# A decoder block in fp32: the convolution's shifted copies through DRAM, second operands and layer-norm factors in PSUM banks, no layer-norm end on GpSimd

## The chip, the cores and the metric

The kernel runs on one core of a Trainium2 chip. The metric is the device time of one execution in microseconds (us); the lower, the better.

## The reference, cut to what matters

One decoder layer over 256 tokens of 2048 channels, in fp32. The part that the change touches is the mixing sub-layer, where one input projection feeds two groups.

```python
z = rms_norm(x) @ w_in                       # 2048 -> 3360 + 2 * 1024 columns
# RWKV group: every column is shifted, z + (prev - z) * mu, then r, k, v of 8 pairs of heads
kk = kk / max(sqrt(sum(kk * kk)), 1e-12)     # norm of the keys, per head
y = wkv7_scan(...)                           # the recurrence; then group norm, gain, bias, bonus, gate
# convolution group
u = u_lin * sigmoid(u_gate)                  # 1024 channels
c = depthwise_conv(u, width 31) + dw_b
c = (c - mean(c)) * rsqrt(var(c) + 1e-5) * ln_gain + ln_bias     # over the channels
y_conv = c * sigmoid(c)
mixed = concat(y, y_conv) @ w_out            # then a residual, an MLP of 8192, an embedding gate
```

## The kernel before, in words

All activations lie transposed, channels on the partitions and the 256 tokens along the free axis. A matrix product of a weight tile (128 output channels, 16 blocks of 128 input channels) is made of three fp32r products: weight and activation are each split into a high and a low part. SP's queue loads 1 MB of weights into one of two buffers `W`; in four quarters ScalarE casts the high part `wh` (L285), and mostly GpSimd subtracts it to get the low part `wl` (L248); TensorE runs the tile (L434 to L442) into one of two PSUM banks `acc`. A tile of w_in is 48 matmuls.

The work is written as generators that ask for buffers (`Take`) and issue operations; a planner (`Plan.run`) with a cost for each operation decides the order on every engine while the program is built, and engine queues keep this order. An operation releases its buffers when it is through. Operations may name two engines, of which the planner takes the one that is done first (`PD` and `DP` are GpSimd or VectorE). Tiles of w_in have a low priority and fill TensorE between the pieces of the eight pairs of heads. `ORDER` places the tiles of the pairs and of eight convolution blocks (128 channels each; one tile `lin`, one `gate`). After the last convolution block comes the layer norm over all 1024 channels, while the tiles of the last pairs still run; then w_out's convolution half, while the last recurrences run; then w_out's other half. At about 510 us the mixing is over, and the MLP follows.

What the change and the prediction speak of, with the lines before:

- `scaled` and `zshift` (L614 to L632): a tile leaves its bank `acc` by a multiplication with the row norm on VectorE into `zp`, which frees the bank; ScalarE writes `(1 - mu) * z` into `zt` in SBUF, and VectorE joins both, with two SBUF operands.
- `keys` (L691 to L722): norms of the keys in `n4`, and their copy `rn` (L714), SBUF to SBUF.
- `inverse`: the small sums `ud` (L838) of each pair, in SBUF.
- `recur` and `group_norm` (L972 to L1002): the recurrence's output is copied by ScalarE from its bank `psy` into `ysb`, and normed from there.
- `ev_gate` (L1021): the gate times `u`, two SBUF operands, on GpSimd or VectorE.
- `taps` (L1034): the block's `u` (128 channels, 3 zeros and 256 tokens) is brought into four groups of 32 channels, each in four shifts on four groups of partitions, by 16 matmuls with columns of the identity (L1044) into two banks `wk`, which ScalarE copies into the one buffer `cv` (L285). 32 matmuls then make the convolution (L1056).
- `layer_norm` (L1065): mean (L1070), squares, variance (L1082), then `1 / sqrt` into `csq` (L1084), and for each block the multiplication by `csq`, gain and bias, a sigmoid on ScalarE and the last product, on GpSimd or VectorE and from SBUF alone.

Of the kernel before, what the change touches and what calls it, by code (L numbers as in the profile page):

```python
# [16 lines left out]
P = 128  # L17
# [37 lines left out]
TAP, LNP, AFP = 4.0, 1.0, 3.5  # L55
# [42 lines left out]
class Plan:  # L98
# [100 lines left out]
    def issue(self, task, best):  # L199
# [123 lines left out]
def decoder_block(ctx: ExitStack, tc: tile.TileContext, x, p, w_in, w_gd, w_out, w_up, w_down,  # L323
# [225 lines left out]
    pl.static("cv", cvst)  # L549
    def v4(t):  # L550
# [63 lines left out]
    def scaled(acc, o, W, cols=P):  # L614
        yield Wait(lambda: "rstd" in S)
        r = S["rstd"]
        yield pl.tt(["DVE"], o, acc.t[:cols, :T], r.t[:cols], ALU.mult, T, [acc, r], [W], [acc])

    def zshift(acc, o, W, mu, j=0, cols=P):
        zp = yield Take("zp", 1)  # L620
        yield pl.memset(zp.t[:, 0:1], 0.0, [(zp, 0)], 1)
        yield from scaled(acc, zp.t[:cols, 1:], zp, cols)
# [69 lines left out]
    def keys(j):  # L692
# [12 lines left out]
        n4 = yield Take("n4")  # L705
        yield pl.ts(["DVE"], n4.t, psn.t[:, 0:4], 1e-24, None, ALU.max, None, 4, [psn], [n4], [psn])
# [88 lines left out]
    def bonus(j):  # L795
# [4 lines left out]
        yield pl.stt(rk.t, zr.t, vec("r_k", j), kp.t, ALU.mult, ALU.mult, T, [zr, kp], [rk], [zr, kp])  # L800
# [713 lines left out]
```

## Time and profile before

| what | us |
|---|---|
| median of 3 runs | 1400.93 (1400.87 to 1402.88) |
| the profiled execution | 1402.03 |
| its span, first to last instruction | 1400.2 |
| TensorE busy | 1351.5 (97%) |
| GpSimd busy | 1174.2 (84%) |
| ScalarE busy | 799.4 (57%) |
| VectorE busy | 736.4 (53%) |

The profiled execution took 1.8 us more than its span and lies 1.1 us above the median. A busy share is over the whole span; what binds a stage is read from the stage's windows, the waits and the chain. TensorE's clock has two levels here, 1.2 and 2.4 GHz; the profile gives the mean as a share of the upper one.

### The profile page before, as it was taken

The numbers are of one execution on the slowest core, as the hardware profiler recorded it, in microseconds if no ns is written. First come the engines' busy times: TensorE is split into PE (matmuls) and PEld (weight loads), VectorE is DVE, ScalarE is ACT, GpSimd is POOL, SyncE is SP. The second block draws the span as 40 slices with busy tenths as digits, with TensorE's granted clock in tenths as the row PEclk, the third lists the DMA queues.
The fourth block names the chain that finished last, engine by engine and source line by source line (L and its number), as shares of the span: only waits on it lengthen the run. The fifth ranks groups of instructions, "written<-read, shape, count | busy, mean of one in ns | idle before, by whom it ended". The sixth has DMA issues, their size and how long they took to land.

```text
span 1400.2 us, 27458 instructions
## 1 busy us (share of the span) xinstructions
PE 1351.5 (97%) x10476; PEld 1182.8 (84%) x10476; DVE 736.4 (53%) x1305; ACT 799.4 (57%) x1667; POOL 1174.2 (84%) x1002
## 2 busy tenths in 40 slices
PE   8999999999789999999999999999999999999898
PEld 7868878788778998788888888888888888889688
DVE  7256837235886545687003663236632266433694
ACT  6835665556657656855445554455554455555853
POOL 7765756576777769789999999999999999999787
PEclk9999999999899999999999999999999999999999
DMA  7442333433222465345555554555554555555353
GB/s 243 159 140 95 115 130 113 137 110 137 91 99 95 153 248 182 128 160 194 211 182 191 194 185 181 183 189 194 187 181 182 187 194 189 181 181 190 124 198 120
DMA packets 40354, 229.40 MB, mean 164 GB/s; under 512 B 6304, under 2 KB 9632, under 8 KB 14624
## 3 DMA queue, kind: packets, MB, share of 16 engines
q1 hardware_dynamic: 40224, 227.66, 46.0%
q8 instruction: 82, 1.34, 0.4%
q14 instruction: 48, 0.39, 0.1%
HBM read 225.55 MB, written 2.10 MB: 163 GB/s over the span
## 4 chain that ended last, share of the span: by engine, by line
PE 86%; DVE 8%; ACT 2%; issue 1%; DMA 1%; POOL 1%; SPq 0%; DVEq 0%; ACTq 0%; POOLq 0%
PE acc L441 34%; PE acc L442 17%; PE acc L434 8%; PE acc L435 7%; PE acc L436 7%; PE acc L440 3%; PE inv L1056 2%; PE acc L439 1%; PE wk L1044 1%; DVE hl L252 1%; DVE acc L246 1%; DVE acc L252 1%; PE psy L930 1%; PE seq L938 1%; PE wk L749 1%
## 5 line engine op out<-in xcount | busy, mean ns | idle before, releaser
L248 POOL TENSOR_TENSOR wl<-W,wh 128x512 fp32r<-128x512 f32 x548 | 734.4, 1353 | 119.2 <-ACT wh L285 99.3
L285 ACT CAST wh<-W 128x512 fp32r<-128x512 f32 x568 | 346.3, 618 | 220.3 <-PE acc L440 69.0
L441 PE MATMUL acc<-hl,wh 128*128 128x512 f32 x1016 | 369.8, 403 | 11.3 <-DVE hl L252 5.7
L441 PE MATMUL acc<-fhl,wh 128*128 128x512 f32 x806 | 288.2, 395 | 0.0
L442 PE MATMUL acc<-hl,wl 128*128 128x256 f32 x1016 | 286.5, 282 | 0.0
L434 PE MATMUL acc<-hl,wh 128*128 128x256 f32 (+1 forms) x928 | 282.1, 304 | 1.0 <-DVE zp L246 0.9
L436 PE MATMUL acc<-hl,wl 128*128 128x256 f32 (+1 forms) x928 | 265.2, 286 | 6.3 <-POOL wl L248 6.0
L435 PE MATMUL acc<-hl,wh 128*128 128x256 f32 (+1 forms) x928 | 265.7, 286 | 3.2 <-DVE hl L252 2.0
L248 POOL TENSOR_TENSOR wl<-Wb,wh 128x512 fp32r<-128x512 f32 x173 | 237.0, 1380 | 18.4 <-ACT wh L285 11.2
L441 PEld LDWEIGHTS acc<-hl,wh 128*128 128x128 f32 x1016 | 192.1, 189 | 60.2 <-DVE hl L252 8.4
L442 PE MATMUL acc<-fhl,wl 128*128 128x256 f32 x806 | 227.2, 282 | 0.0
L442 PEld LDWEIGHTS acc<-hl,wl 128*128 128x128 f32 x1016 | 193.2, 190 | 3.7
L434 PEld LDWEIGHTS acc<-hl,wh 128*128 128x128 f32 (+1 forms) x928 | 179.2, 193 | 15.6 <-issue 10.1
L246 DVE TENSOR_TENSOR gt<-acc,tb 128x256 f32<-128x256 f32 x124 | 52.4, 423 | 263.7 <-ACT tb L276 263.1
L436 PEld LDWEIGHTS acc<-hl,wl 128*128 128x128 f32 (+1 forms) x928 | 179.1, 193 | 7.3 <-POOL wl L248 6.6
L435 PEld LDWEIGHTS acc<-hl,wh 128*128 128x128 f32 (+1 forms) x928 | 179.5, 193 | 5.4 <-DVE hl L252 3.7
L441 PEld LDWEIGHTS acc<-fhl,wh 128*128 128x128 f32 x806 | 151.5, 188 | 33.4
L285 ACT CAST wh<-Wb 128x512 fp32r<-128x512 f32 x174 | 107.6, 621 | 89.4 <-PE acc L440 35.5
L442 PEld LDWEIGHTS acc<-fhl,wl 128*128 128x128 f32 x806 | 151.3, 188 | 2.7
L246 DVE TENSOR_TENSOR f<-f 128x256 f32<-128x256 f32 x63 | 85.9, 1366 | 1.9
L246 DVE TENSOR_TENSOR fhl<-f,fhl 128x256 fp32r<-128x256 f32 x62 | 58.5, 946 | 26.0 <-ACT fhl L276 26.0
L248 POOL TENSOR_TENSOR wlb<-W,whb 128x512 fp32r<-128x512 f32 x50 | 69.2, 1384 | 1.9 <-ACT whb L285 1.6
(319 smaller groups left out, 2004.2 us busy)
## 6 DMA issues: line engine op xcount, KB each, us to landing
W<-in_w_up_dram SPq DMA_DIRECT2D x43, 1024.0 KB, 4.8
W<-in_w_down_dram SPq DMA_DIRECT2D x42, 1024.0 KB, 4.8
W<-in_w_in_dram SPq DMA_DIRECT2D x38, 1024.0 KB, 4.9
Wb<-in_w_down_dram SPq DMA_DIRECT2D x22, 1024.0 KB, 4.8
Wb<-in_w_up_dram SPq DMA_DIRECT2D x21, 1024.0 KB, 4.8
W<-in_w_out_dram SPq DMA_DIRECT2D x14, 1024.0 KB, 4.8
W<-in_w_gate_dram SPq DMA_DIRECT2D x11, 1024.0 KB, 5.0
Wb<-in_w_gate_dram SPq DMA_DIRECT2D x5, 1024.0 KB, 4.8
```

What stands on the lines that cost most here:

```text
L246: alts.append((e, dve, lambda: nc.vector.tensor_tensor(out=out, in0=a, in1=b, op=op), None, pen))
L248: alts.append((e, 220 + 2.27 * n, lambda: nc.gpsimd.tensor_tensor(out=out, in0=a, in1=b, op=op), None, pen))
L252: return Op([("DVE", 210 + 1.042 * n + (0 if self.from_psum(R) or n < 128 else PORT), lambda: self.nc.vector.scalar_tensor_tensor(out=out, ...
L285: alts.append((e, 150 + 0.835 * n, lambda: self.nc.scalar.copy(out, a), None, 0))
L434: return [nc.tensor.matmul(o, h, xk[:, 0, :], start=(i == 0), stop=False), nc.tensor.matmul(o, h, xk[:, 1, :], start=False, stop=False), n ...
L435: nc.tensor.matmul(o, h, xk[:, 1, :], start=False, stop=False),
L436: nc.tensor.matmul(o, l, xk[:, 0, :], start=False, stop=(i == n - 1))]
L439: return [nc.tensor.matmul(a[:cols, T:], l, xk[:, 0, :], start=False, stop=False), nc.tensor.matmul(a[:cols, :], h, both, start=False, sto ...
L440: nc.tensor.matmul(a[:cols, :], h, both, start=False, stop=True)]
L441: return [nc.tensor.matmul(a[:cols, :], h, both, start=(i == 0), stop=False), nc.tensor.matmul(a[:cols, T:], l, xk[:, 0, :], start=False, ...
L442: nc.tensor.matmul(a[:cols, T:], l, xk[:, 0, :], start=False, stop=False)]
L1056: nc.tensor.matmul(ps.t[32 * g:32 * g + 32, :T], cw.t[:, g, m, :], cv.t[:, g, 4 * m:4 * m + T], start=(m == 0), stop=(m == 7)) for g in ra ...
```

## The change

Three things, all between about 60 and 510 us. **The copies:** `taps` no longer uses TensorE and ScalarE to spread `u`; one DMA writes `u` into a buffer in DRAM, and four DMAs read it back, shifted, into `cv`, 40 DMAs in all on SP's queue. The planner charges SP 600 ns for each and 4 us and more until it lands, instead of 60 ns and 330 ns for loads (330 ns now). **Second operands in PSUM:** of two operands on VectorE one now mostly lies in a bank: the shift's second half in the upper half of the tile's own `acc`, the sigmoid of the gate likewise, `psy` directly instead of `ysb`, the bonus joined in a bank, `n4` and `ud` in banks. So banks are held longer: `acc` until the shift is done, `wk` of the norms until `rn` is written, `inv` from the sums on, `wk` instead of `psy` in the group norm. **The end of the layer norm:** the reciprocal goes into the bank `pv`; eight multiplications by it on VectorE; then sigmoid (into a bank `wk`) and gain and bias (in place) both on ScalarE, and the last product on VectorE with the sigmoid in the bank. GpSimd has no part in it. Instructions in all: TensorE 9115 to 8987 (the 128 of L1044), ScalarE 1635 to 1615, GpSimd 1002 to 994, VectorE 1305 to 1309, SP's DMAs 266 to 306.

```diff
@@ Plan.issue
         if eng == "DMA":
-            self.clock["SP"] = st + 60
-            self.dma = max(self.dma, st + 700) + c
-            en = self.dma + 1900
+            self.clock["SP"] = st + (func or 330)
+            if func:
+                en = max(self.dma, st + 700) + c + 3300
+            else:
+                self.dma = max(self.dma, st + 700) + c
+                en = self.dma + 1900
@@ scaled, zshift
-        yield pl.tt(["DVE"], o, acc.t[:cols, :T], r.t[:cols], ALU.mult, T, [acc, r], [W], [acc])
+        yield pl.tt(["DVE"], o, acc.t[:cols, :T], r.t[:cols], ALU.mult, T, [acc, r], [W], [] if keep else [acc])
-        d = yield Take("zt", 1)
-        yield pl.act(d.t[:cols], zp.t[:cols, 1:], AF.Identity, T, [zp, "omu"], [d], scale=om)
-        a, b = zp.t[:cols, 0:T], d.t[:cols]
+        d = acc.t[:cols, T:]
+        yield pl.act(d, zp.t[:cols, 1:], AF.Identity, T, [zp, "omu"], [(acc, "d")], scale=om)
+        a, b = zp.t[:cols, 0:T], d
...
-        yield pl.stt(o, a, mu, b, ALU.mult, ALU.add, T, [d, zp, (zp, 0), "vt"], [W], [d, zp])
+        yield pl.stt(o, a, mu, b, ALU.mult, ALU.add, T, [(acc, "d"), zp, (zp, 0), "vt"], [W], [acc, zp])
@@ keys
-        n4 = yield Take("n4")
-        yield pl.ts(["DVE"], n4.t, psn.t[:, 0:4], 1e-24, None, ALU.max, None, 4, [psn], [n4], [psn])
+        n4, kn = psn.t[:, 4:8], (psn, "n")
+        yield pl.ts(["DVE"], n4, psn.t[:, 0:4], 1e-24, None, ALU.max, None, 4, [psn], [kn])
...
-        yield pl.vec(202, lambda: nc.vector.tensor_copy(rn.t, n4.t[:, :, None].to_broadcast([P, 4, C])),
-                     [n4], [rn], [n4])
+        yield pl.vec(202, lambda: nc.vector.tensor_copy(rn.t, n4[:, :, None].to_broadcast([P, 4, C])),
+                     [kn], [rn], [psn])
@@ inverse
-        ud = yield Take("ud")
+        pe = yield Take("inv")
+        ud, kd = pe.t[:, T:T + 32].rearrange("p (c j) -> p c j", c=NC), (pe, "t")
...
@@ recur, group_norm
-        yield pl.copy(["ACT"], ysb.t.rearrange("p a t -> p (a t)"), psy.t[:, :T], T, [(psy, False), (psy, True)], [ysb], [psy])
-        pl.spawn(group_norm(j, ysb), 1.1)
+        pl.spawn(group_norm(j, psy), 1.1)
...
-        yield pl.tt(["DVE"], cen.t, ysb.t, s4.t[:, :, None].to_broadcast([P, 4, C]), ALU.subtract, T,
-                    [ysb, s4], [cen], [s4])
+        yield pl.tt(["DVE"], cen.t, yv, s4.t[:, :, None].to_broadcast([P, 4, C]), ALU.subtract, T,
+                    ky + [s4], [cen], [s4, psy])
...
-        pgn = yield Take("psy")
+        pgn = yield Take("wk", 2)
...
-        yield pl.stt(y.t[:, j, :], bv.t, vec("gn_bias", j), gs.t, ALU.add, ALU.mult, T, [bv, gs], [(y, j)], [bv, gs])
+        yield pl.stt(y.t[:, j, :], pgn.t[:, T:], vec("gn_bias", j), gs.t, ALU.add, ALU.mult, T, [(pgn, 1), gs], [(y, j)], [pgn, gs])
@@ ev_gate
-            yield pl.act(gt.t, gt.t, AF.Sigmoid, T, [gt], [gt])
+            yield pl.act(acc.t[:, T:], gt.t, AF.Sigmoid, T, [gt], [(acc, "d")], [gt])
...
-            yield pl.tt(PD, lin, lin, gt.t, ALU.mult, T, [gt, u], [u], [gt])
+            yield pl.tt(["DVE"], lin, lin, acc.t[:, T:], ALU.mult, T, [(acc, "d"), u], [u], [acc])
@@ taps
-        for b in range(2):
-            pr = yield Take("wk")
-            for g in (2 * b, 2 * b + 1):
-                o = (g % 2) * T
-                yield pl.pe(600, lambda: [
-                    nc.tensor.matmul(pr.t[32 * i:32 * i + 32, o:o + T], ident[:, 32 * g:32 * g + 32],
-                                     u.t[:, i:i + T], start=True, stop=True) for i in range(4)],
-                            [u, (u, 0), "fc"], [pr], [u] if g == 3 else [])
-            yield pl.copy(["ACT"], cv.t[:, 2 * b:2 * b + 2, 28:], pr.t.rearrange("p (g t) -> p g t", g=2), 2 * T,
-                          [pr], [(cv, b)], [pr])
+        ur = yield Take("ur")
+        yield pl.dma_move(ur.t, u.t, P * (3 + T) * 4, [u, (u, 0)], [ur], [u])
+        for i in range(4):
+            yield pl.dma_move(cv.t[32 * i:32 * i + 32, :, 28:], ur.t[:, i:i + T].rearrange("(g c) t -> c g t", g=4),
+                              P * T * 4, [ur], [(cv, i)] + [cv] * (i == 0), [ur] if i == 3 else [])
@@ layer_norm
-        yield pl.act(csum, pv.t[:, :T], AF.Sqrt, T, [pv], ["csum"], [pv], bias=bias_cache[LN_EPS])
-        yield pl.vec(1669, lambda: nc.vector.reciprocal(csq, csum), ["csum"], ["crs"])
+        yield pl.act(csum, pv.t[:, :T], AF.Sqrt, T, [pv], ["csum"], bias=bias_cache[LN_EPS])
+        rp, kr = pv.t[:, T:], (pv, "r")
+        yield pl.vec(1669, lambda: nc.vector.reciprocal(rp, csum), ["csum"], [kr])
...
-                yield pl.tt(DP, a, a, csq, ALU.mult, T, ["crs", (y, NP + j, "m")], [k])
-                yield pl.ts(DP, a, a, vec("ln_g", j), vec("ln_b", j), ALU.mult, ALU.add, T, [k], [k])
-                g = yield Take("sqt")
-                yield pl.act(g.t, a, AF.Sigmoid, T, [k], [g])
-                yield pl.tt(PD, a, a, g.t, ALU.mult, T, [k, g], [(y, NP + j)], [g])
...
+            lg = yield Take("wk")
+            yield pl.act(lg.t[:, :T], a, AF.Sigmoid, T, [k], [lg], scale=vec("ln_g", j), bias=vec("ln_b", j))
+            yield pl.act(a, a, AF.Identity, T, [k], [(y, NP + j, "l")], scale=vec("ln_g", j), bias=vec("ln_b", j))
+            yield pl.tt(["DVE"], a, a, lg.t[:, :T], ALU.mult, T, [(y, NP + j, "l"), lg], [(y, NP + j)], [lg])
...
+            yield pl.tt(["DVE"], a, a, rp, ALU.mult, T, [kr, (y, NP + j, "m")], [(y, NP + j, "n")], [pv])
```

The planner writes another order with it. Three places matter below. The first is SP's queue at the first convolution block (`cw` are the block's taps, `gup` weights of a pair, `ur` the buffer in DRAM, `cvst` is `cv`), before and then with the change:

```order
L231 DMA cw<-in_w_cv_dram 128x1024
L231 DMA W<-in_w_in_dram 128x2048 x2
L231 DMA gup<-in_w_gup_dram 128x256
L231 DMA W<-in_w_in_dram 128x2048
```

```order
L234 DMA cw<-in_w_cv_dram 128x1024
L234 DMA W<-in_w_in_dram 128x2048
L234 DMA gup<-in_w_gup_dram 128x256
L237 DMA ur<-u 128x259
L234 DMA W<-in_w_in_dram 128x2048
L237 DMA cvst_111<-ur 32x4x256 x4
L234 DMA W<-in_w_in_dram 128x2048
```

The write to DRAM waits in the queue for `u`, and the four reads wait for the write to land; one weight load stands between them, and the next one behind them.

The second is TensorE at the third convolution block, with the change. `acc_2160` is the bank of its gate tile, `acc_2320` and `acc_2499` those of the next two tiles; the rows on `seq` are a recurrence, those on `X` and `U` a pair's inverse:

```order
L441 MATMUL acc_2160<-hl_121,wh_2182 128x256
L442 MATMUL acc_2160<-hl_121,wl_2183 128x256
L440 MATMUL acc_2320<-hl_121,wh_2216 128x256
...
L886 MATMUL inv_2444<-X_2434,U_2139 32x32 x16
L946 MATMUL seq_2457<-SV_1775,arK_1598 128x128
...
L442 MATMUL acc_2499<-hl_121,wl_2450 128x256
L1059 MATMUL inv_2637<-cvst0_111,cw_2294 32x256 x4
L952 MATMUL seq_2703<-rh_2705,xbst0_110 128x64
L1059 MATMUL inv_2637<-cvst0_111,cw_2294 32x256 x8
```

Between the end of the gate tile and the first convolution matmul (L1059) stand 81 matmuls of tiles and pieces of the pairs; at the other seven blocks it is more. The copying matmuls are gone.

The third is GpSimd at the end of the layer norm, before and then with the change (`wl` are weight splits), and VectorE there with the change:

```order
L248 TENSOR_TENSOR wl<-W,wh 128x512
L248 TENSOR_TENSOR y<-y,csq 128x256
L265 TENSOR_SCALAR y<-y,vt 128x256
L248 TENSOR_TENSOR y<-y,csq 128x256 x3
L248 TENSOR_TENSOR y<-y,sqt 128x256
L265 TENSOR_SCALAR y<-y,vt 128x256
L248 TENSOR_TENSOR y<-y,sqt 128x256 x3
L291 MEMSET zp 128x1
L248 TENSOR_TENSOR arK<-zr,Ep 64x4x64
L248 TENSOR_TENSOR BK<-kp,Em 64x4x64
L248 TENSOR_TENSOR wl<-W,wh 128x512 x2
```

```order
L254 TENSOR_TENSOR wl<-W,wh 128x512
L254 TENSOR_TENSOR cen<-cen,s_5047 128x256
L254 TENSOR_TENSOR wl<-W,wh 128x512 x3
L297 MEMSET zp 128x1
L254 TENSOR_TENSOR wl<-W,wh 128x512 x3
L297 MEMSET Ep 128x4
```

```order
L1088 RECIPROCAL wk<-csum 128x256
L258 SCALAR_TENSOR_TENSOR wk<-wk,vt,bv 128x256
L252 TENSOR_TENSOR y<-y,wk 128x256 x8
L258 SCALAR_TENSOR_TENSOR y<-wk,vt,gs 128x256
L252 TENSOR_TENSOR zp<-acc,rstd 128x256
```

The ten pieces of the layer norm that stood between the weight splits are gone from GpSimd's queue; on VectorE the eight multiplications stand in one block ahead of the next tile's `zp`.

## Rows read from the trace of the kernel before

**Rows 1.** Page, part 1 (busy us, share of the span, instructions of two engines) and part 2 (one character for each of 40 slices of 35 us; PEclk in tenths of full speed).

```profile
PE 1351.5 (97%) x10476; PEld 1182.8 (84%) x10476; DVE 736.4 (53%) x1305; ACT 799.4 (57%) x1667; POOL 1174.2 (84%) x1002
...
PEclk9999999999899999999999999999999999999999
```

**Rows 2.** Busy time of each engine in three windows of 35 us, from the end of the convolution's tiles to the start of w_out's (us from the span's start, length, then each engine's busy us with its instructions, the granted clock, the DMA engines' busy share, GB/s).

```profile
350.00:385.00 35.00, 26.25 (x210) 24.69 (x209) 31.41 (x54) 21.57 (x47) 26.28 (x33) 0.87 0.26 91
385.00:420.00 35.00, 30.21 (x356) 27.29 (x356) 30.66 (x71) 19.90 (x46) 27.54 (x31) 0.98 0.28 99
420.00:455.00 35.00, 32.18 (x422) 29.81 (x420) 21.29 (x61) 26.21 (x67) 27.07 (x32) 0.90 0.27 95
```

**Rows 3.** Page, part 4: the chain that ended last, shares of the span by engine.

```profile
PE 86%; DVE 8%; ACT 2%; issue 1%; DMA 1%; POOL 1%; SPq 0%; DVEq 0%; ACTq 0%; POOLq 0%
```

**Rows 4.** Groups of TensorE instructions over the whole span (line, operation, out<-in, shape, count | busy us, mean ns of one | idle just before, releaser). A matrix product in fp32 is two records.

```profile
L1044 PE MATMUL wk<-u,fc 128*32 128x256 f32 x256 | 19.1, 395 | 1.9 <-DVE bv L246 1.9
L1056 PE MATMUL inv<-cvst,cw 128*32 128x256 f32 x512 | 31.8, 383 | 0.0
L878 PE MATMUL inv<-X,U 32*32 32x32 f32 x512 | 7.3, 194 | 0.2 <-ACT cvst L285 0.2
```

**Rows 5.** TensorE in order of time around the first convolution's copies (start us, us, instruction, in brackets the idle time before it and who ended it). Between the first two rows shown lie 36 more matmuls of tiles.

```profile
62.05 0.28 PE L434 MATMUL acc<-hl,wh 128*128 128x256 f32 x1
...
66.48 0.28 PE L435 MATMUL acc<-hl,wh 128*128 128x256 f32 x1
...
73.83 0.64 PE L1044 MATMUL wk<-u,fc 128*32 128x256 f32 x8
...
75.03 0.64 PE L1044 MATMUL wk<-u,fc 128*32 128x256 f32 x8
...
78.80 1.52 PE L1044 MATMUL wk<-u,fc 128*32 128x256 f32 x16 [1.87 <-DVE bv L246]
```

**Rows 6.** Busy time in windows of 5 us, the same columns as in group 2: two at the first convolution's copies, four at the end of the layer norm.

```profile
75.00:80.00 5.00, 3.13 (x34) 1.75 (x33) 3.70 (x4) 1.10 (x2) 4.27 (x4) 0.93 0.14 49
80.00:85.00 5.00, 5.00 (x57) 3.89 (x57) 1.50 (x4) 2.44 (x5) 3.53 (x4) 0.73 0.14 21
370.00:375.00 5.00, 3.46 (x39) 3.06 (x37) 3.56 (x10) 2.47 (x7) 5.00 (x7) 1.00 0.01 2
375.00:380.00 5.00, 1.86 (x7) 1.57 (x7) 5.00 (x6) 1.01 (x3) 4.73 (x6) 0.62 0.09 16
380.00:385.00 5.00, 3.69 (x18) 3.70 (x19) 4.68 (x9) 4.92 (x9) 2.30 (x5) 0.50 0.54 193
385.00:390.00 5.00, 4.42 (x34) 3.97 (x34) 2.19 (x5) 4.08 (x10) 0.57 (x1) 0.85 0.01 2
```

**Rows 7.** TensorE at the end of the layer norm, in order of time.

```profile
377.52 0.58 PE L436 MATMUL acc<-hl,wl 128*128 128x256 f32 x1 [4.06 <-POOL wl L248]
```

**Rows 8.** GpSimd at the end of the layer norm, in order of time.

```profile
364.57 1.29 POOL L248 TENSOR_TENSOR wl<-W,wh 128x512 fp32r<-128x512 f32 x1
365.81 0.92 POOL L248 TENSOR_TENSOR y<-y,csq 128x256 f32<-128x256 f32 x1
...
372.62 2.13 POOL L248 TENSOR_TENSOR y<-y,sqt 128x256 f32<-128x256 f32 x3
...
376.21 2.67 POOL L248 TENSOR_TENSOR wl<-W,wh 128x512 fp32r<-128x512 f32 x2
```

**Rows 9.** Groups of VectorE instructions between 0 and 510 us, columns as in group 4. The first four read two operands in SBUF, the last two one in SBUF and one in a PSUM bank.

```profile
L252 DVE SCALAR_TENSOR_TENSOR zk<-zp,vt,zt 128x256 f32<-128x256 f32 x8 | 6.1, 758 | 6.2 <-ACT zt L277 5.5 <-POOL csq L248 0.7
L252 DVE SCALAR_TENSOR_TENSOR zr<-zp,vt,zt 128x256 f32<-128x256 f32 x8 | 5.9, 734 | 1.7 <-ACT zt L277 1.7
L252 DVE SCALAR_TENSOR_TENSOR vd<-zp,vt,zt 128x256 f32<-128x256 f32 x8 | 7.1, 886 | 0.8 <-ACT zt L277 0.7
L252 DVE SCALAR_TENSOR_TENSOR y<-bv,vt,gs 128x256 f32<-128x256 f32 x8 | 7.2, 901 | 0.2
L252 DVE SCALAR_TENSOR_TENSOR bv<-psy,vt,bv 128x256 f32<-128x256 f32 x8 | 3.9, 482 | 5.2 <-PE psy L994 5.1
L246 DVE TENSOR_TENSOR y<-y,wk 128x256 f32<-128x256 f32 x8 | 3.3, 411 | 0.4 <-PE wk L1070 0.4
```

**Rows 10.** The copy of the key norms from SBUF to SBUF, among the instructions on tile rn (count, ns shortest/median/longest, first and last start).

```profile
L714 DVE COPY rn<-n x8: 293/468/1394, 69.9 to 418.3; 128x256 f32<-128x256 f32 x8
```

**Rows 11.** VectorE in order of time: the two steps of one token shift.

```profile
367.80 0.40 DVE L246 TENSOR_TENSOR zp<-acc,rstd 128x256 f32<-128x256 f32 x1
...
379.91 0.47 DVE L252 SCALAR_TENSOR_TENSOR vd<-zp,vt,zt 128x256 f32<-128x256 f32 x1
```

**Rows 12.** DMA issues on SP's queue (count, KB each, median us from issue to landing).

```profile
out_dram<-os SPq DMA_DIRECT2D x16, 128.0 KB, 1.8
gup<-in_w_gup_dram SPq DMA_DIRECT2D x8, 128.0 KB, 5.1
pt<-in_p_dram SPq DMA_DIRECT2D x1, 256.0 KB, 9.8
```

**Rows 13.** The first convolution's gate tile: VectorE's first step on it and GpSimd's last, in order of time.

```profile
69.52 0.42 DVE L246 TENSOR_TENSOR gt<-acc,rstd 128x256 f32<-128x256 f32 x1 [0.99 <-PE acc L436]
...
71.06 0.69 POOL L248 TENSOR_TENSOR u<-u,gt 128x256 f32<-128x256 f32 x1
```

More of the change, by code (lines that the diff above doesn't have):

```diff
@@ L549, in decoder_block @@
     pl.static("cv", cvst)
+    dr = pa.enter_context(tc.tile_pool(name="dr", bufs=2, space=bass.MemoryType.DRAM))
+    reg(dr, "ur", 2, [P, 3 + T])
     def v4(t):
@@ L612, in x_norm, with scaled @@
         yield pl.act(warm, bias_cache[1e-6], AF.Sigmoid, 1, (), ["warm"])
-    def scaled(acc, o, W, cols=P):
+    def scaled(acc, o, W, cols=P, keep=False):
         yield Wait(lambda: "rstd" in S)
         r = S["rstd"]
-        yield pl.tt(["DVE"], o, acc.t[:cols, :T], r.t[:cols], ALU.mult, T, [acc, r], [W], [acc])
+        yield pl.tt(["DVE"], o, acc.t[:cols, :T], r.t[:cols], ALU.mult, T, [acc, r], [W], [] if keep else [acc])
     def zshift(acc, o, W, mu, j=0, cols=P):
@@ L621, in zshift @@
         yield pl.memset(zp.t[:, 0:1], 0.0, [(zp, 0)], 1)
[L622 removed]
+        yield from scaled(acc, zp.t[:cols, 1:], zp, cols, True)
         mu, om = vec(mu, j, rows=cols), omu[:cols, VOFF[mu] + j if VOFF[mu] < 24 else 24 + VOFF[mu] - VOFF["mu_wa"] + j:][:, 0:1]
[L624 to L626 removed]
+        d = acc.t[:cols, T:]
+        yield pl.act(d, zp.t[:cols, 1:], AF.Identity, T, [zp, "omu"], [(acc, "d")], scale=om)
+        a, b = zp.t[:cols, 0:T], d
         if len(o.shape) == 3:
             a, b = ck(a), ck(b)
[L629 removed]
+        yield pl.stt(o, a, mu, b, ALU.mult, ALU.add, T, [(acc, "d"), zp, (zp, 0), "vt"], [W], [acc, zp])
     def ev_wa(acc):
@@ L836, in inverse @@
                     m8[:, None, :, None].to_broadcast(sh), ALU.mult, T, Uk + ["fc"], [um])
-        ud = yield Take("ud")
-        yield pl.vec(335, lambda: nc.vector.tensor_reduce(out=ud.t, in_=um.t.rearrange("p c q j -> p c j q"),
-                                                          axis=mybir.AxisListType.X, op=ALU.add), [um], [ud], [um])
+        pe = yield Take("inv")
+        ud, kd = pe.t[:, T:T + 32].rearrange("p (c j) -> p c j", c=NC), (pe, "t")
+        yield pl.vec(555, lambda: nc.vector.tensor_reduce(out=ud, in_=um.t.rearrange("p c q j -> p c j q"),
+                                                          axis=mybir.AxisListType.X, op=ALU.add), [um], [kd], [um])
         udh = yield Take("udh")
         udl = yield Take("udl")
-        yield pl.copy(["DVE"], udh.t, ud.t, 32, [ud], [udh])
-        yield pl.tt(["DVE"], udl.t, ud.t, udh.t.bitcast(F32), ALU.subtract, 32, [ud, udh], [udl], [ud])
+        yield pl.copy(["DVE"], udh.t, ud, 32, [kd], [udh])
+        yield pl.tt(["DVE"], udl.t, ud, udh.t.bitcast(F32), ALU.subtract, 32, [kd, udh], [udl])
         es = []
@@ L1023, in f @@
             gt = yield Take("gt")
-            yield from scaled(acc, gt.t, gt)
-            yield pl.act(gt.t, gt.t, AF.Sigmoid, T, [gt], [gt])
+            yield from scaled(acc, gt.t, gt, keep=True)
+            yield pl.act(acc.t[:, T:], gt.t, AF.Sigmoid, T, [gt], [(acc, "d")], [gt])
             yield Wait(lambda: "u" in cvs[j])
@@ L1057, in taps @@
                                  start=(m == 0), stop=(m == 7)) for g in range(4)],
-                        [cw, (cv, 0), (cv, 1)], [ps], [cw, cv] if m == 7 else [])
+                        [cw] + [(cv, i) for i in range(4)], [ps], [cw, cv] if m == 7 else [])
         yield pl.act(a, ps.t[:, :T], AF.Identity, T, [ps], [ka], [ps], bias=vec("dw_b", j))
```

40 lines of the change are left out of this document (21 added, 19 removed).

## The prediction

> **What bounds the kernel now.** I read the page's shares and slices first, then the chain, then windows of the stages that the diff touches, and last the waits in them.
>
> TensorE is busy 97% of the span [rows 1], and it makes up 86% of the chain that ended last, VectorE 8% and GpSimd 1% [rows 3]. So a matmul that goes away is worth its time wherever TensorE runs without a gap, and another engine's work is worth something only where TensorE waits for it. It waits in few places. The worst stretch is 350 to 455 us [rows 2]: TensorE is busy 26.25, 30.21 and 32.18 of 35 us, so 16.4 us are lost to gaps, while VectorE is at 31.4 and 30.7 of 35 in the first two windows. There the layer norm ends beside the last tiles of w_in.
>
> The heart of it is 370 to 390 us [rows 6]. Idle are 1.54, 3.14, 1.31 and 0.58 us, together 6.6. After the gap the granted clock is 0.62, 0.50 and 0.85 of full speed (0.50 is the lower level, 1.2 GHz). Busy time at a lower clock loses its missing share: 1.86 x 0.38 + 3.69 x 0.50 + 4.42 x 0.15 = 3.2 us. That makes 9.8 us. The longest wait in it is one of 4.06 us for a weight split `wl` on GpSimd [rows 7], and GpSimd shows why [rows 8]: its last split before began at 364.57, then it worked on layer-norm pieces and two pieces of a pair from 365.81, and the next split began at 376.21, 11.6 us later.
>
> **The change, part by part.** The sum is made against the profiled execution, 1402.0 us, which is 1.1 above the median of the runs; I leave that difference alone, since the runs spread over 2 us.
>
> *The copying matmuls go.* The group L1044 holds TensorE for 19.1 us [rows 4], from 73.83 us on [rows 5]. They stand in the gapless row of tiles, which follow one another every (66.48 - 62.05) / 37 = 0.120 us; what stood behind them moves up. I take **-19.1 us**. With them goes a wait of 1.87 us for a bank `wk` [rows 5]; the clock of 0.93 and 0.73 behind it costs 3.13 x 0.07 + 5.00 x 0.27 = 1.6 us more [rows 6]. I take **-1.9** and keep 0 and -3.5 as the ends, since another wait may stand there. The 16 copies on ScalarE that also go cost nothing now: no chain share shows them [rows 3].
>
> *The DMAs that replace them.* Forty issues go onto SP's queue, ahead of weight loads. No transfer through DRAM is in the trace. The nearest rows are 128 KB each: the output at 1.8 us, alone, and `gup` at 5.1 us, behind weight loads [rows 12]. A write and a read one after the other take 3.6 to 10.2 us. The cover is shortest at the third block: 81 tile matmuls at 0.120 make 9.7 us, 80 small ones of the inverse, 160 records at 7.3 / 512 us each [rows 4], 2.3 us more; the gate's way from bank to finished `u`, from 69.52 to 71.75 [rows 13], takes 2.2 off. That leaves 9.8 us, not counting the recurrence's pieces. At worst each of eight blocks waits 0.4 us. I take 0, with +3 as the upper end. A weight load held back behind the reads has two buffers and seven split quarters (`NW`, `NH`) ahead of it; if that cover were gone, it would come on top.
>
> *The layer norm's end leaves GpSimd.* The ten pieces between the splits go, so the split that TensorE waited 4.06 us for comes in time. At most the 9.8 us above go, at least nothing: VectorE, nearly full there, gets sixteen multiplications. They read a bank, and such a one takes 411 ns [rows 9], 6.6 us in all, less than the mix of before. I take **-7**, about the idle time with little of the clock.
>
> *Second operands in banks.* The shift's three forms and the gating take 758, 734, 886 and 901 ns with both operands in SBUF; the same operation with one operand in a bank takes 482 [rows 9]. Over eight pairs that is 8 x (0.276 + 0.252 + 0.404 + 0.419) = 10.8 us of VectorE. Only what TensorE waits for counts: at least nothing, at most the 7.0 us of idle time that 390 to 455 us hold ([rows 2] less the last window of [rows 6]). I take **-2**, near the low end, since those waits are short and have several causes. For the copy `rn` the operand moves the other way: from SBUF it takes 293 ns at its shortest, 468 in the middle and 1394 at its longest [rows 10]; from a bank the nearest row is 411 [rows 9], so 8 copies cost +0.9 us by the shortest and -0.5 by the median. I take 0. *The Trainium skill (VectorE: DVE Perf Modes, "Why PSUM operands drop a tier") says that an fp32 operand in PSUM loses the double rate that a copy from SBUF can have. By that rule alone `rn` is slower with the change and the sum 0.9 us worse; the row's median says that the fast form is mostly not what this kernel gets.*
>
> *Banks are held longer.* This is the price. A tile's bank was free after `zp`; now it is held until the shift is done. Just such a pair of steps began at 367.80 and ended at 380.38, 12.6 us [rows 11], where a tile takes 48 x 0.120 = 5.7 us; with two banks TensorE would stand still for 6.9 us. With the change eight multiplications stand ahead of one `zp`, 8 x 0.411 = 3.3 us. At least nothing, at most 6.9; I take **+3**, by that block.
>
> Sum: -19.1 - 1.9 - 7 - 2 + 3 = **-27.0**, so 1402.0 - 27.0 = **1375.0 us**. With all the good ends, -19.1 - 3.5 - 9.8 - 7 = -39.4, 1363; with all the bad ones, -19.1 + 3 + 6.9 = -9.2, 1393.
>
> **The rivals.** *The banks eat the gain of the layer norm.* TensorE no longer waits for splits there, but for `acc` and `wk`, of which the layer norm now holds one until its eighth multiplication. For it: VectorE's 90% in [rows 2]. Against it: VectorE's operations get shorter just there. Price: -7 and -2 fall away and 6.9 come, -21.0 + 6.9 = -14.1, 1388 us.
>
> *Everything shortens.* If the waits on VectorE between 390 and 455 us go with the contention, and the clock stays up, it is the good end, 1363. Against it: in order, each engine will find its next latest operand.
>
> *TensorE is not the bound after all.* If the pairs' chains or VectorE set the pace, the 19.1 us turn into gaps and little more than the layer norm's 7 us is left, 1395; or nothing, 1402. Against it: all windows outside of 350 to 455 us would have to show gaps like those in [rows 2], and 97% busy leaves no room for them.
>
> *The way through DRAM is late, and the kernel slower.* The place is the first convolution matmul of each block, and the weight loads queued behind the reads. Against the 9.8 us of cover, each landing above 4.9 us costs twice its excess, eight times over. The gain of 27 us is gone when both take 4.9 + 27 / 16 = 6.6 us. One row says that this can be: `pt`, 256 KB among other loads, 9.8 us [rows 12]; at that each block waits 9.8 us, and it would be 1375 + 78 = 1453. Against it: the eight loads of the right size, in the same stage, have a median of 5.1.
>
> *The change doesn't do what it says* where an operation with one operand in a bank is stretched by GpSimd all the same. The two bank rows of [rows 9], 482 and 411 ns on average over eight each, speak against that, and I give it no chance of its own.
>
> **How the numbers follow.** The forecast has a chance of 0.60, the banks 0.20, the good end 0.08, TensorE not the bound 0.05, DRAM too late 0.07. The range from 1363 to 1392 takes in the first three, less what lies at their edges. A measurement of this kernel can tell 0.2%, 2.8 us, from no change. Faster by more than that: 0.60 + 0.20 + 0.08 and 0.02 of the fourth, 0.90. Within it: the other 0.03 of the fourth. Slower: 0.07.
>
> **What would show it.** Right: no L1044 copies, TensorE's busy time down by about 19 us, DRAM reads that land before L1059 without a wait there; at the layer norm's end no gap of 4 us for `wl`, and the clock at 1.00; the shift's three forms near 480 ns. The layer norm begins about 20 us earlier, the MLP about 27. Wrong: waits of TensorE or its weight loads for `cvst`, for a weight load behind the reads, or for `acc` held by a shift; VectorE without a gap for 30 us behind the variance, with TensorE idle for more than 10 of them.

## The result, and the profile after

The changed kernel takes **1368.2 us** (median of 4 runs, 1367.8 to 1369.4), beside 1401.9 us for the kernel before in the same session: ratio 0.9759, 95% interval 0.9742 to 0.9776, so 33.7 us less. The profiled execution took 1369.4 us with a span of 1367.5. The forecast was 1375.0 with a range from 1363 to 1392: the sign and the range hold, and the size is 7 us short. The terms behind it fit less well, as the runs below show.

The page after, its parts 1, 2 and 4, beside [rows 1, 3]:

```profile
PE 1328.4 (97%) x10220; PEld 1176.2 (86%) x10220; DVE 713.3 (52%) x1309; ACT 791.1 (58%) x1647; POOL 1159.9 (85%) x994
...
PEclk9999999999989999999999999999999999999999
...
PE 85%; DVE 6%; ACT 4%; DMA 2%; issue 1%; POOL 1%; SPq 0%; DVEq 0%; ACTq 0%; POOLq 0%
```

TensorE has 256 instructions and 23.1 us less, and is as full as before. The span fell by 32.7 us, so some 10 us of idle time went besides. The windows of [rows 2], after:

```profile
350.00:385.00 35.00, 28.88 (x328) 26.89 (x328) 25.48 (x68) 29.22 (x55) 15.83 (x23) 0.90 0.23 77
385.00:420.00 35.00, 32.01 (x354) 29.86 (x353) 29.94 (x81) 26.02 (x66) 30.27 (x38) 0.92 0.23 84
420.00:455.00 35.00, 35.00 (x524) 32.88 (x524) 20.64 (x64) 22.65 (x59) 26.32 (x23) 0.98 0.44 156
```

TensorE is busy 95.9 of 105 us instead of 88.6, and GpSimd in the first window 15.8 instead of 26.3 us. Still there are gaps, and the granted clock is down to 0.90 again in the first window. What TensorE waited for in the first 560 us (total, times, longest us):

```profile
PE acc L447 <- DVE hl L258: 5.7, 6, 2.8
PE wk L777 <- DVE y L252: 5.3, 2, 4.4
PE acc L440 <- DVE wa L258: 2.9, 1, 2.9
...
PE wk L757 <- DVE y L252: 2.0, 1, 2.0
...
PE inv L1059 <- DMA cvst<-ur: 1.3, 1, 1.3
```

The wait for a split of [rows 7] is gone. In its place TensorE waits 4.4 us for a bank `wk` (L777, a pair's transposes). It doesn't wait behind VectorE's eight multiplications by the reciprocal: they run from 356.5 to 359.2 us, and TensorE has no gap between 346.4 and 368.4. What holds the two banks `wk` are the layer norm's sigmoids: each block's lies in a bank until the block's last product has read it. The rows of TensorE, ScalarE and VectorE there:

```profile
372.83 0.27 PE L777 MATMUL wk<-fc,BK 64*128 64x64 f32 x1 [4.41 <-DVE y L252]
...
363.17 1.28 ACT L283 ACT_TABLE_LOAD   x1
364.46 0.42 ACT L283 ACTIVATE Ep<-L 128x256 f32<-128x256 f32 x1
...
365.27 1.28 ACT L283 ACT_TABLE_LOAD   x1
366.56 0.57 ACT L283 ACTIVATE wk<-y,vt 128x256 f32<-128x256 f32 x1
...
372.35 0.42 DVE L252 TENSOR_TENSOR y<-y,wk 128x256 f32<-128x256 f32 x1 [0.39 <-ACT y L283]
```

ScalarE makes the eight sigmoids (`wk<-y,vt`) between 360.6 and 372.8 us, two before and six behind a break for an exponential of a pair (`Ep`), with a table load of 1.28 us on either side of it. The transposes get their first bank when the seventh product, at 372.35, has freed it.

Of the waits in the first 560 us, the third row is for a bank held by the first shift, the last the only one for a DRAM read; none is for a weight load behind the reads. The groups of VectorE from 0 to 510 us, columns as in [rows 9]:

```profile
L252 DVE TENSOR_TENSOR y<-y,wk 128x256 f32<-128x256 f32 x24 | 9.4, 416 | 2.9 <-ACT y L283 2.7
L258 DVE SCALAR_TENSOR_TENSOR y<-wk,vt,gs 128x256 f32<-128x256 f32 x8 | 3.8, 480 | 0.1
L258 DVE SCALAR_TENSOR_TENSOR zk<-zp,vt,acc 128x256 f32<-128x256 f32 x8 | 3.8, 479 | 2.6 <-ACT acc L283 2.5
L722 DVE COPY rn<-wk 128x256 f32<-128x256 f32 x8 | 3.3, 418 | 0.2
L258 DVE SCALAR_TENSOR_TENSOR zr<-zp,vt,acc 128x256 f32<-128x256 f32 x7 | 3.3, 477 | 1.5 <-ACT acc L283 1.4
L258 DVE SCALAR_TENSOR_TENSOR vd<-zp,vt,acc 128x256 f32<-128x256 f32 x7 | 3.3, 477 | 2.6 <-ACT acc L283 2.6
L252 DVE TENSOR_TENSOR u<-u,acc 128x256 f32<-128x256 f32 x8 | 3.3, 416 | 5.4 <-ACT acc L283 5.4
```

The shift's three forms and the gating are at 477 to 480 ns, from 734 to 901. And the transfers through DRAM, beside [rows 12]:

```profile
cvst<-ur SPq DMA_DIRECT2D x32, 128.0 KB, 5.9
ur<-u SPq DMA_DIRECT2D x8, 129.5 KB, 2.1
```

### The profile page after: what moved, and what is told of

It is laid out like the page before. It is cut to its first block, busy times and chain, and to the rows that moved or that the text cites. A ratio compares the mean times of both kernels' runs of the same rounds, so it can differ in the third digit from the quotient of the medians.

```text
span 1367.5 us, 27001 instructions
## 1 busy us (share of the span) xinstructions
PE 1328.4 (97%) x10220; PEld 1176.2 (86%) x10220; DVE 713.3 (52%) x1309; ACT 791.1 (58%) x1647; POOL 1159.9 (85%) x994
## 4 chain that ended last, share of the span: by engine, by line
PE 85%; DVE 6%; ACT 4%; DMA 2%; issue 1%; POOL 1%; SPq 0%; DVEq 0%; ACTq 0%; POOLq 0%
PE acc L447 35%; PE acc L448 18%; PE acc L440 8%; PE acc L441 7%; PE acc L442 7%; PE acc L446 3%; PE inv L1059 2%; PE acc L445 1%; DVE hl L258 1%; ACT L283 1%; DVE acc L252 1%; DVE acc L258 1%; PE seq L946 1%; DMA mac<-in_x_dram 1%; ACT wh L291 1%
## 5 line engine op out<-in xcount | busy, mean ns | idle before, releaser
L447 PE MATMUL acc<-hl,wh 128*128 128x512 f32 x1045 | 376.0, 400 | 9.9 <-DVE hl L258 5.7
L447 PE MATMUL acc<-fhl,wh 128*128 128x512 f32 x837 | 297.2, 395 | 0.0
L448 PE MATMUL acc<-hl,wl 128*128 128x256 f32 x1045 | 294.4, 282 | 0.0
L447 PEld LDWEIGHTS acc<-hl,wh 128*128 128x128 f32 x1045 | 197.6, 189 | 58.5 <-DVE hl L258 8.3
L448 PE MATMUL acc<-fhl,wl 128*128 128x256 f32 x837 | 235.5, 281 | 0.0
L448 PEld LDWEIGHTS acc<-hl,wl 128*128 128x128 f32 x1045 | 198.8, 190 | 3.1
L447 PEld LDWEIGHTS acc<-fhl,wh 128*128 128x128 f32 x837 | 157.3, 188 | 34.7
L448 PEld LDWEIGHTS acc<-fhl,wl 128*128 128x128 f32 x837 | 157.1, 188 | 2.9
```

The source lines that it names most:

```text
L447: return [nc.tensor.matmul(a[:cols, :], h, both, start=(i == 0), stop=False), nc.tensor.matmul(a[:cols, T:], l, xk[:, 0, :], start=False, ...
L448: nc.tensor.matmul(a[:cols, T:], l, xk[:, 0, :], start=False, stop=False)]
```

## The experiments

Two chains run side by side up to the last half tiles of w_out: TensorE's tiles, and the eight pairs, whose last result the rest of w_out needs. The runs are read by the end of each: when the last half tile was stored (last `mac<-acc`), and when TensorE began the last pair's transposes for the group norm (an expectation's 505.0 is VectorE's step before them). The last column is how long the last pair's bonus held a bank `wk`, from its matmul to VectorE's multiplication that frees it (`bv<-vd,wk`). Times are us. The kernel before was at 1401.7 to 1402.5 in all sessions.

| Kernel | Median | Ratio to before, 95% interval | Tiles end | Last pair | Bank held |
|---|---|---|---|---|---|
| before | 1401.9 | | 503.0 | 506.7 | 19.7 |
| changed | 1368.2 | 0.9742 to 0.9776 | 474.4 | 470.7 | 1.5 |
| e1 copies | 1393.3 | 0.9921 to 0.9951 | 479.0 | 498.5 | 35.1 |
| e2 norm's end | 1409.3 | 1.0036 to 1.0066 | 495.8 | 513.7 | 30.2 |
| e3 second operands | 1394.0 | 0.9925 to 0.9958 | 493.4 | 498.5 | 4.3 |
| e4 changed, first shift in SBUF | 1371.5 | 0.9763 to 0.9795 | 473.7 | 470.1 | 1.6 |
| e5 copies, norm's end, two lines | 1375.3 | 0.9792 to 0.9826 | 481.5 | 483.2 | 3.9 |
| e6 changed, two lines put back | 1363.8 | 0.9707 to 0.9747 | 466.2 | 465.6 | 8.2 |
| e7 two lines | 1402.8 | 0.9994 to 1.0016 | 501.3 | 507.6 | 3.3 |
| e8 changed, old norm's end | 1369.7 | 0.9748 to 0.9784 | 474.2 | 470.5 | 2.6 |
| e9 copies, one line | 1379.1 | 0.9816 to 0.9845 | 484.2 | 483.9 | 0.6 |
| e10 copies, two lines | 1379.6 | 0.9820 to 0.9851 | 487.2 | 488.8 | 1.0 |
| e11 e6, first shift in SBUF | 1369.2 | 0.9736 to 0.9776 | 471.9 | 471.2 | 8.2 |
| e12 changed, two hops | 1375.3 | 0.9769 to 0.9827 | 480.6 | 477.0 | 1.7 |

**The three parts, each alone (e1 to e3).** Each run is the kernel before with the hunks of the diff that belong to one part: the copies through DRAM, the layer norm's end, or all bank operands.

> The kernel before with the DRAM copies alone. Theory (the three parts add up as in the prediction's sum, with the stage of the convolutions undersized): 19.1 us of matmuls and 1.9 us of a wait go, and up to 5 us more, since first to last gate fell by 25.8 us with the whole change; -21 to -26 us, 1376 to 1381 against a median of 1401.9, TensorE's busy time down by 19. Rival 1 (the 5 us more are VectorE's, from the gating with a bank operand): -17 to -21. Rival 2 (the copies were not on the path, another engine holds the stage): less than -10.

> The kernel before with the new end of the layer norm alone. Theory (the prediction's term): the 4.06 us wait for `wl` at 377.5 goes with its low clock, -7 us, at most -9.8. Rival 1 (the multiplications with a bank only shorten when the shifts around them do too, so the term needs the bank operands of the other part): 0 to -3. Rival 2 (the held `wk` bank and VectorE's queue cost what the splits give): 0 to +7.

> The kernel before with the bank operands alone (shift, keys, bonus, inverse, group norm, gating). Theory (the prediction's -2, and a price of about +5 for banks held at the start): between -2 and +4. Rival 1 (VectorE's shorter operations carry what was measured beyond the copies and the layer norm): -5 to -10, with 650 us of shift forms gone on the shift, and fewer gaps between 350 and 455 us. Rival 2 (banks held cost more than that without the copies' room): +4 or more.

Measured: -9.1, +6.9 and -8.4 us, each where a rival had put it: rival 2 for the copies and for the layer norm's end, rival 1 for the operands. They add up to -10.6, and together they give -33.7: more than two thirds of the gain is in none of the parts. The table tells where it is lost. With the copies alone the tiles end 24.0 us earlier, as the theory said, but the last pair only 8.2 us earlier; TensorE has run out of tiles and waits, as its window from 480 to 520 us shows:

```profile
480.00:520.00 40.00, 32.28 (x252) 30.54 (x251) 19.43 (x41) 18.15 (x44) 18.96 (x15) 0.83 0.47 173
```

7.7 us idle, and the clock at 0.83. With the layer norm's end alone the tiles end 7.2 us earlier, again as forecast, and the last pair 7.0 us *later*. TensorE in order of time with the copies alone, cut to the bonus of the last pair (L810), the group norm of the pairs before it (L1002) and the chunk products of the last pair (L757):

```profile
417.00 0.82 PE L810 MATMUL wk<-rk,fc 128*128 128x256 f32 x2
...
448.98 0.38 PE L1002 MATMUL psy<-fc,cen 128*128 128x128 f32 x2
452.16 1.57 PE L757 MATMUL wk<-arK,BK 64*128 64x128 f32 x16
454.84 0.38 PE L1002 MATMUL psy<-fc,cen 128*128 128x128 f32 x2
498.48 0.69 PE L1002 MATMUL psy<-fc,cen 128*128 128x128 f32 x2 [3.78 <-POOL cen L254]
```

and VectorE there:

```profile
449.40 0.48 DVE L258 SCALAR_TENSOR_TENSOR bv<-psy,vt,bv 128x256 f32<-128x256 f32 x1 [0.27 <-PE psy L1002]
...
450.26 1.59 DVE L258 SCALAR_TENSOR_TENSOR y<-bv,vt,gs 128x256 f32<-128x256 f32 x1
...
452.11 0.41 DVE L252 TENSOR_TENSOR bv<-vd,wk 128x256 f32<-128x256 f32 x1
```

Read it backwards. The chunk products need both `wk` banks. One is the bonus's, written at 417.0 and read at 452.1, since the bonus of before takes its bank first and then asks for one of the two `bv` buffers. That buffer came free at 451.9 (450.26 + 1.59) with the group norm of the pair two before, whose transposes wanted the bank `psy`, and this the pair between had for its recurrence until 448. So a bank lay idle for 35.1 us and the last pair behind it. With the layer norm's end alone the same rows stand 13.5 to 18.5 us later (bonus 435.46, multiplication 465.67, products 465.71). I call this the bank knot. The bank operands carry two lines that bear on it:

```
-        pb = yield Take("wk")              (bonus: bank, then bv)
-        bv = yield Take("bv")
+        bv = yield Take("bv")              (first bv, then the bank)
+        pb = yield Take("wk")
...
-        pgn = yield Take("psy")            (group norm's transposes)
+        pgn = yield Take("wk", 2)
```

**The first shift (e4).** The shift of the first tiles frees its bank after `zp` again, by a buffer `zt` where `j == 0` or the tile is the short one:

```
+        sb = j == 0 or cols < P
-        yield from scaled(acc, zp.t[:cols, 1:], zp, cols, True)
+        yield from scaled(acc, zp.t[:cols, 1:], zp, cols, not sb)
...
+            zt = yield Take("zt", 1)       (if sb: d is zt; else acc.t[:cols, T:])
```

> The changed kernel with the shift of the first tiles (wa, k0, r0, v0 and the two of gd) put back into SBUF, so that their bank is free after `zp`. Theory (the price of banks held longer falls at the start, where the first gate came 5.3 us later than before, behind a wait of 2.9 us for `acc` at 42 us): -3 to -5 us against the changed kernel's 1368.2, and the first gate near 70 us. Rival (the start is later since the plan is another one, or since the slack is taken back behind it): within 1.5 us of the changed kernel, the first gate at 73 us or later.

The first gate began at 69.4 us, against 74.8 with the change and 69.5 before, so the price of the held bank at the start is real. The end gained nothing (1368.6 to 1373.7 in the runs). Its windows from 75 to 200 us:

```profile
75.00:130.00 55.00, 51.76 (x646) 43.61 (x645) 36.07 (x90) 28.29 (x65) 37.07 (x42) 1.00 0.45 137
130.00:200.00 70.00, 67.00 (x898) 61.04 (x896) 43.47 (x120) 43.05 (x97) 47.31 (x54) 1.00 0.45 151
```

TensorE does 118.8 us of work there where the changed kernel does 53.9 + 70.0 = 123.9: the 5 us are taken back. The expectation's rival was right that nothing comes of it, though the median is 3.3 us above the changed kernel's and not within 1.5; it had the start wrong.

**The bank knot (e5 to e7, e9, e10).** e5 has the copies, the layer norm's end and the two lines, with no second operand in a bank; e6 is the changed kernel without the two lines; e7 is the kernel before with them alone.

> The kernel before with the DRAM copies, the new end of the layer norm, and of the bank operands only two lines: the group norm's transposes go to a bank `wk` instead of `psy`, and the bonus takes its buffer `bv` before it takes its bank. No second operand is moved into a bank. Theory (two chains run side by side up to the last half tiles of w_out, TensorE's tiles and the pairs; what the copies and the layer norm give the tiles came to nothing in the first runs since the last pair's bonus held one of two `wk` banks for 35.1 us, waiting for `bv`, and these lines undo that): the tiles' -24 and -7 come through, 1369 to 1376, and the bonus's bank is held for less than 5 us. Rival (the shorter operations of VectorE are what lets the pairs keep up): 1385 to 1393, with the last pair as late as before.

> The changed kernel with only those two lines as they were: transposes of the group norm in `psy`, the bonus's bank taken before `bv`. Theory (bank knot): the last pair is late again by 15 to 35 us against tiles that end at 474, so TensorE idles at the end of that stage as with the copies alone; 1380 to 1393. Rival (VectorE's shorter operations carry it): within 4 us of the changed kernel's 1368.

> The kernel before with those two lines alone. Theory (the end is the later of the two chains; in the kernel before the last half tile of w_out began at 503.0 us and the last group norm's transposes at 505.0, so with the pairs early only the tiles bound): 0 to -3 us, the last pair's transposes more than 10 us earlier. Rival 1 (TensorE also gains from pieces of pairs that come earlier): -5 to -9, as with all the bank operands. Rival 2 (a transposition in `wk` takes a bank from the pairs): 0 to +5.

e5 came at 1375.3: two lines turn a sum of -9.1 + 6.9 = -2.2 into -26.4. e7 gave nothing measurable, though for another reason than expected: the chunk products of the last pair moved only from 455.5 to 454.3, so the hold of 19.7 us in the kernel before was not what kept them. And e6 went against me: without the two lines the changed kernel is not 12 to 25 us slower but 4.4 us **faster**, the fastest version here (its runs took 1362.1 to 1366.8 us, the changed kernel's 1367.8 to 1369.4; the intervals of the two ratios overlap by a sliver). The rows show why the knot does not bind there:

```profile
405.90 0.70 PE L810 MATMUL wk<-rk,fc 128*128 128x256 f32 x2
413.07 0.44 PE L1002 MATMUL psy<-fc,cen 128*128 128x128 f32 x2
414.53 1.24 PE L757 MATMUL wk<-arK,BK 64*128 64x128 f32 x16
...
465.57 0.38 PE L1002 MATMUL psy<-fc,cen 128*128 128x128 f32 x2
```

The group norm got `psy` before the next recurrence took it, and the bank is held 8.2 us instead of 35.1. By these rows the knot is a race for `psy` that each plan decides anew: it binds with the copies or the layer norm's end over SBUF operands (e1, e2), and not in e6 with the operands in banks. What e6 gains over the changed kernel stands in part at the layer norm: its eight sigmoids follow one another from 355.9 to 365.3 us without the break, and the wait of 4.4 us is one of 1.3. That the two lines as such bring the break about is not shown. Which line undoes it:

> The kernel before with the DRAM copies and one line more: the bonus takes its buffer `bv` before its bank `wk`; the group norm's transposes stay in `psy`. Theory (what held the last pair back with the copies alone is the `wk` bank that its bonus held for 35.1 us, from 417.0 to 452.1, with one bank left for the two that the chunk products need): the tiles' -24 us come through, 1375 to 1382, and the last pair's chunk products begin before 440 us. Rival (the group norm's wait for `psy` is the hold, the bank only goes with it): 1390 to 1395, chunk products at 450 or later.

> The kernel before with the DRAM copies and the two lines of the bank knot, without the new end of the layer norm. It weighs the layer norm's end where VectorE's operands are still in SBUF: with it, this was 1375.3 us. Theory (its 7 us are there wherever the shifts are stretched, and go where the bank operands shorten them, as the changed kernel lost only 1.5 us without it): 1380 to 1384. Rival (it is worth little in either, since the wait for `wl` is replaced by one for the bank that `y` holds): 1375 to 1378.

One line takes the copies from -9.1 to -23.3 us. The same rows of TensorE as above, with it (L811 is the bonus):

```profile
433.61 1.16 PE L757 MATMUL wk<-arK,BK 64*128 64x128 f32 x16
449.71 0.38 PE L1002 MATMUL psy<-fc,cen 128*128 128x128 f32 x2
450.86 0.59 PE L811 MATMUL wk<-rk,fc 128*128 128x256 f32 x2
...
483.94 0.38 PE L1002 MATMUL psy<-fc,cen 128*128 128x128 f32 x2
```

The group norm's transposes come as late as before (449.7), since they still wait for `psy`; but the bonus now comes behind them, and the chunk products no longer wait: 433.6 instead of 452.2, and the last pair is 14.5 us earlier. That is the theory's case, and the rival's (`psy` alone holds) falls. The second line adds nothing to it (e10); alone it was not run.

**The layer norm's end (e8, with e5 and e10).** e8 is the changed kernel with the hunks of `layer_norm` undone.

> The changed kernel with the end of the layer norm as it was before. Theory (with the knot undone the parts add: the layer norm's term is worth the 7.2 us by which the tiles ended earlier with it alone): 1375 to 1378. Rival (the copies and the bank operands already gave all, the wait for `wl` at the layer norm is overlapped by the pairs): within 2 us of 1368.

It lost 1.5 us, within the runs' spread, so the rival held in size; the wait for `wl` is gone as it said, though another has taken its place. TensorE's longest waits between 315 and 420 us, in e8, then in the kernel before and with the copies alone:

```profile
PE acc L440 <- DVE zr L258: 4.9, 1, 4.9
PE wk L757 <- DVE y L252: 2.0, 1, 2.0
...
PE acc L436 <- POOL wl L248: 6.0, 3, 4.1
...
PE acc L440 <- DVE zp L252: 3.9, 1, 3.9
```

With the old end TensorE waits 4.9 us for a bank `acc` that a shift holds, with the new one 4.4 for a bank that the sigmoids hold. The wait for `wl` of the kernel before is not there with either: the copies alone leave 1.1 us of it, and TensorE waits 3.9 for `acc` instead, behind VectorE's `zp`. Where the operands are in SBUF the new end is worth 1379.6 - 1375.3 = 4.3 us (e10 against e5), between both expectations; it trades a wait of 6.4 us for `acc` for one of 3.9 for the sigmoids' bank. Neither size is clear of what the planner's order alone can do: e6, which differs from the change by two allocations, moved by 4.4 us. TensorE's busy time from 350 to 455 us sorts it: 89.1 of 105 in e10, 91.3 with the norm's end (e5), 95.2 with the operands (e8), 95.9 with both, and 99.3 in e6.

**The best version, and the cover of the DRAM way (e11, e12).** e11 joins e6 and e4. e12 makes the write to DRAM two: `ur.t[:, 0]` from `u`, `ur.t[:, 1]` from `ur.t[:, 0]`, and reads the second, with the order on every engine otherwise unchanged.

> The changed kernel with the two lines of the bank knot put back, which was 1363.8 us, and the first tiles' shift in SBUF, which had moved the first gate 5.4 us up without moving the end. Theory (the time is set by the pairs' chain and the tiles together, so an earlier start is taken back between 80 and 160 us again): 1362 to 1366. Rival (the two add up): 1358 to 1361.

> The changed kernel with one more copy in DRAM between the write and the four reads of each block, in the same plan and order of every engine. One hop more is at least the 2.1 us of a write's landing. Theory (the cover is all but used up: from the end of `u` to the first convolution matmul the changed kernel has 10.8 to 13.0 us, and a write of 2.1, four issues of 2.1 and a read's 5.9 make 10.1 of them, with one wait of 1.3 us): eight waits of some 1 to 3 us on L1061 and +6 to +20 us. Rival 1 (TensorE takes the lost time back, since it waits elsewhere for the pairs anyway): waits there, but less than +5. Rival 2 (the reads' landing time is mostly queueing behind weight loads that run dry meanwhile, so a later issue lands as early): no waits, within 1.5 us.

e11 missed both: 1369.2, by the medians 5.4 us slower than e6, though the intervals of their ratios overlap. First to last gate take 240.3 us where e6 takes 233.4, so the start, 3.5 us earlier, is paid back twice; which wait does that I did not find. e12 costs 7.1 us by the medians, as the theory's time said (its runs took 1370.9 to 1378.6 us, so that size is rough), but not by its waits: TensorE waits for the reads three times, 1.6 us together. From the added hop's 2.8 us the reads won back 0.9:

```profile
cvst<-ur SPq DMA_DIRECT2D x32, 128.0 KB, 5.0
ur<-u SPq DMA_DIRECT2D x8, 129.5 KB, 1.9
ur<-ur SPq DMA_DIRECT2D x8, 129.5 KB, 2.8
```

First to last gate grew by 6.8 us (233.8 to 240.6). 1.6 of it is those waits; another is one of 1.8 for a pair's `BK`, and the rest lies in small gaps. How a later read brings those about stays open.

## Why the prediction was right, and where it was not

- *The copying matmuls and the wait behind them, -21.0.* Right in size once the pairs can follow: -23.3 in e9, and between first and last gate 241.6 instead of 259.5 us, -17.9. What failed is the step "what stood behind them moves up". With nothing else only 9.1 us came out, since the pairs did not move up with the tiles. They can with the change's line on `bv` (e9), which the prediction did not price, or with the operands in banks without that line (e6), which it took for a small gain.
- *DMAs through DRAM, 0.* It came out at one wait of 1.3 us, but by two errors that cancel. From the finished `u` to the landing of the last read went 9.2 to 12.9 us, since the four reads of a block are issued one after the other, some 1.6 us from the first to the last, which the prediction left out; its cover of 9.8 us would have been short in six of the eight blocks. The cover was 10.8 to 12.6 us, with the pieces of the recurrence in it that the prediction didn't count. It is not ample: in the seven blocks without a wait the last read landed 0.5 to 2.7 us before the first matmul that reads it, and one hop more cost some 7 us.
- *The layer norm's end, -7.* This step failed in the changed kernel. With the layer norm's end alone the forecast mechanism is there: TensorE's waits for `wl` between 315 and 420 us go from 6.0 to 0.5 us, and the tiles end 7.2 us earlier (e2). But with the copies the wait for `wl` has already given way to one for `acc` (all but 1.1 us in e1, all in e8 and e10), so the new end had no such wait to remove. It took away a wait for `acc` and brought the sigmoids' 4.4 us for `wk`: -1.5 us in this kernel (e8), -4.3 without the bank operands. The clock there was 0.90, not 1.00 as forecast.
- *Second operands, -2.* Mis-sized the other way: 1379.6 - 1369.7 = 9.9 us (e10 against e8) and 1375.3 - 1368.2 = 7.1 (e5 against the change). I counted the idle time of 390 to 455 us only. But the operands alone also shorten first to last gate from 259.5 to 252.3 us (e3), where VectorE was thought to be off the path. The operations did take the forecast 480 ns.
- *Banks held longer, +3.* The place named, the block of eight multiplications, cost nothing: TensorE had no gap while it ran. The layer norm does make TensorE wait for a bank, but by the sigmoids, which the sum has no term for; that wait is what leaves the layer norm's term at -1.5 and would be counted twice. A bank `acc` held by a shift did cost 4.9 us at the old end of the layer norm (e8), and in the change 2.9 us at the start, behind `wa`, with the first gate 5.3 us later. e4 took that away and the end did not move, so as a term of its own this one is 0.
- *The copy `rn`.* 418 ns on average from a bank. By its shortest, 405 against the 293 of [rows 10], the copy from a bank is slower, as the Trainium skill (VectorE: DVE Perf Modes, "Why PSUM operands drop a tier") has it; but the longest fell from 1394 to 425 and the mean from 667, so VectorE gained all the same.
- *The rivals.* "Banks eat the gain of the layer norm" came true for that term, though by another bank than the one it named, and "everything shortens" for the operands. The two nearly cancel: that a sum with wrong terms came out only 7 us from the time is in part luck. "TensorE is not the bound" was given 0.05, by its 97%; e1 is just that case, with TensorE at 96%.

## What to carry to other kernels

A busy share of 97% did not mean that shorter work on that engine pays in full; here it paid only as far as the next chain followed. So note when each chain ends, here the tiles at 503.0 and the pairs at 506.7, and ask of each part which of the two it moves. Where a task takes a scarce buffer and then waits for another, look for how long the first lies idle (matmul to the operation that frees it); one line in the order of two allocations was worth 14 us here. Parts of a change that meet in such a place must be measured together, since alone one of them even reads as a loss.

## What the runs showed of the hardware

VectorE's operations with one operand in a bank were not stretched, those with two operands in SBUF were. The shift's form `zk` among the instructions on its tile, before and then with the change (count, ns shortest/median/longest, first and last start), and the longest one of before in order of time, with the operation that GpSimd was in:

```profile
L252 DVE SCALAR_TENSOR_TENSOR zk<-zp,vt,zt x8: 483/486/1420, 40.9 to 407.1; 128x256 f32<-128x256 f32 x8
...
L258 DVE SCALAR_TENSOR_TENSOR zk<-zp,vt,acc x8: 473/480/481, 41.8 to 380.4; 128x256 f32<-128x256 f32 x8
...
144.41 1.29 POOL L248 TENSOR_TENSOR wl<-W,wh 128x512 fp32r<-128x512 f32 x1
144.56 1.42 DVE L252 SCALAR_TENSOR_TENSOR zk<-zp,vt,zt 128x256 f32<-128x256 f32 x1
```

The means of 734 to 901 ns in [rows 9] hide two kinds. Of the 32 operations in its first four rows, 16 took 467 to 487 ns. The other 16 took 508 to 1558, and each of them ended 277 to 286 ns after the end of the GpSimd operation that was running when it began (here 145.98 after 145.70). The same forms with one operand in a bank took at most 485 ns, also where GpSimd was in the middle of an operation. The Trainium skill (SBUF — State Buffer, "SBUF: two separate sides") says that a VectorE operation with two SBUF inputs shares a pair of ports with a GpSimd operation that reads SBUF, and that the one that comes second waits until the other is through; these rows agree, and put the price at 1.5 to 1.9 times the operation on average. Of the transfers through DRAM, a read of 128 KB landed in 5.9 us among weight loads of 1 MB, a write of 129.5 KB in 2.1.
